# First norm by channel from a transposed input, its output kept once in DRAM and split on chip

## The chip, the cores and the metric

The kernel runs on one core of one Trainium2 chip. The metric is the device time of one execution in microseconds (us). Shown are the median of the runs and one profiled execution.

## The reference

One layer of a hybrid trunk for 128 context tokens and 2048 latent tokens of width 1024, in float32. What matters here is the start:

```python
h = rmsnorm(x, g_mix) * (1 + scale1) + shift1      # scale1, shift1 from the conditioning vector
p = h @ w_in
qkv, z, a_raw, b_raw, f = jnp.split(p, IN_SPLITS, axis=-1)
qkv = jax.nn.silu(short_conv(qkv, w_conv)).astype(jnp.float32)
```

`rmsnorm` divides each token by the root of the mean of its 1024 squares. `p` has 2576 columns: q, k, v and z with 512 each, 16 for the gates, 512 for a Fourier mixer. Behind it come a chunked gated-delta scan in both directions, the Fourier mixer, an output projection and a gated feed-forward layer.

## The kernel before

**Number format.** A float32 value is split into a high part (rounded, made by a copy on ACT) and a low part (value minus high part, on VectorE), and a product takes three matmuls: high by high, high by low, low by high. `split` (L146) is that pair.

**Layout.** Tokens come in 17 tiles of 128 (16 latent ones, tile 16 is the context), channels in 8 blocks of 128 (`KT`). A projection needs its input with channels on the partitions.

**Stage A** (`phase_a`, L355) goes over the 17 tiles, the context tile first. Per tile it loads x with tokens on the partitions (L383, SP's queue), squares and sums on ACT (`rstd`, L161, with one operation and a power of -1/2 on GpSimd), scales by the result on ACT (`norm`, L283), transposes the eight 128x128 blocks on PE into two PSUM banks, applies the modulation to each block (two of four on VectorE, two on ACT) and splits (`norm_T`, L293). High and low part are stored to DRAM in `hT[2, ...]` (L387 on ACT's queue, L388 on GpSimd's), and 48 matmuls with 528 columns of `w_in`, in two halves, give the gates' inputs and the Fourier input f. The pool `work` holds two buffers each of x, xn, h, hi, lo and f. Weights of the q and k halves are loaded and split in between (`load_halves`); the columns of the modulation come from `mod_columns` ahead of the loop.

**The q/k pass** (`qk_pass`, L550) goes over 8 blocks of 256 latent tokens in the order 0, 7, 1, 6, 2, 5, 3, 4 (`ORDER`); the text numbers blocks by their place in it, 0 to 7. Block 0 has the 128 context tokens beside it. `load_h` (L497) loads a block's high and low parts, with one token more on either side, from `hT` into eight (block 0: sixteen) of the 16 `hb` buffers, one block ahead. A block has eight steps: a projection of 24 matmuls (`project`, L524), a convolution over tokens (`conv_silu`, L535: ACT empties PSUM, VectorE adds the neighbours), and a piece of other work (the modulation of the second norm, `self.mod`; inversions of 64x64 matrices on VectorE by `fill`). Twice per block come the products of q and k.

**The v pass** (`v_pass`, L798) goes over the blocks again, block 7 first, which is still on chip, then 0 to 6, with four projections of v and two or three token tiles of z per block.

**Order.** The program's order is a wish: a scheduler places the instructions on each engine's queue by their dependencies and the buffers that are free. At run time each engine works its queue in order. Three PSUM banks take projections (`acc`), three other matmuls (`m`), two transposes (`tr`).

## Time and profile before

| | us |
|---|---|
| median of 3 runs | 2739.06 (2734.35 to 2741.23) |
| profiled execution | 2737.1 |
| its span, first to last instruction | 2735.3 |
| PE busy in the span | 2619.6 (96%) |
| VectorE (DVE) busy | 1791.5 (65%) |
| ScalarE (ACT) busy | 1412.2 (52%) |

A profile is one execution. PE is TensorE's matmuls, PEld its weight loads, DVE VectorE, ACT ScalarE, POOL GpSimd, SP the queue from which most loads are issued. Matmul records overlap, since matmuls are pipelined, so the distance between two starts is the cost of one. The granted clock is the share of full speed that TensorE was given; 1.0 is 2.4 GHz, and the lower level is 1.2 GHz. "Idle before" is the time in which an engine stood still ahead of an instruction, and the name behind the arrow is what ended it by the records.

### The profile page before, as it was taken

The numbers are of one execution on the slowest core, as the hardware profiler recorded it, in microseconds if no ns is written. First come the engines' busy times: TensorE is split into PE (matmuls) and PEld (weight loads), VectorE is DVE, ScalarE is ACT, GpSimd is POOL, SyncE is SP. The second block draws the span as 40 slices with busy tenths as digits, with TensorE's granted clock in tenths as the row PEclk, the third lists the DMA queues.
The fourth block names the chain that finished last, engine by engine and source line by source line (L and its number), as shares of the span: only waits on it lengthen the run. The fifth ranks groups of instructions, "written<-read, shape, count | busy, mean of one in ns | idle before, by whom it ended". The sixth has DMA issues, their size and how long they took to land.

```text
span 2735.3 us, 45393 instructions
## 1 busy us (share of the span) xinstructions
PE 2619.6 (96%) x16041; PEld 2382.4 (87%) x16041; DVE 1791.5 (65%) x3915; ACT 1412.2 (52%) x3108; POOL 299.5 (11%) x492
## 2 busy tenths in 40 slices
PE   6999999999999999997999999999999999999998
PEld 3898898889888778876999998889999888999986
DVE  6335978618256676667777766487776557888744
ACT  7756656423478877675433344444334444444432
POOL 0211121223200021211000000020000002000001
PEclk8999999999999999999999999999999999999999
DMA  9956788666566666645222223442222254323242
GB/s 311 307 154 197 221 229 225 190 188 187 151 175 193 180 189 180 181 145 174 78 74 70 74 82 123 139 128 74 74 71 71 88 156 140 89 85 89 89 134 93
DMA packets 436112, 396.54 MB, mean 145 GB/s; under 512 B 123084, under 2 KB 359164, under 8 KB 434284
## 3 DMA queue, kind: packets, MB, share of 16 engines
q1 hardware_dynamic: 345132, 297.65, 36.7%
q0 software_dynamic: 16624, 55.85, 6.2%
q10 hardware_dynamic: 74128, 40.13, 5.1%
q8 instruction: 127, 2.08, 0.3%
q14 instruction: 101, 0.83, 0.1%
HBM read 294.74 MB, written 98.79 MB: 144 GB/s over the span
## 4 chain that ended last, share of the span: by engine, by line
PE 73%; DMA 8%; ACT 7%; DVE 6%; issue 4%; POOL 1%; SPq 0%; ACTq 0%; DVEq 0%; POOLq 0%
PE acc L125 24%; PE acc L1304 17%; PE m L1304 16%; PE m L125 15%; DMA hb<-hT 1%; PE tr L128 1%; DMA z_s<-z_d 1%; ACT h L141 1%; ACT bd1r L141 1%; ACT bd0r L141 1%; PE tr L125 1%; ACT u L141 1%; DMA w_raw<-w_in 1%; DMA a_d<-la 1%; DMA hT<-hi 1%
## 5 line engine op out<-in xcount | busy, mean ns | idle before, releaser
L1304 PE MATMUL m<-h,wh 128*128 128x384 f32 (+1 forms) x1848 | 452.2, 327 | 5.5 <-DVE U L131 2.2
L1304 PE MATMUL acc<-h,wh 128*128 128x384 f32 (+1 forms) x1848 | 450.5, 327 | 1.9 <-ACT wh L141 1.9
L141 ACT ACTIVATE wh<-S 128x512 fp32r<-128x512 f32 x264 | 163.3, 630 | 381.4 <-DVE S L131 161.2
L1304 PEld LDWEIGHTS m<-h,wh 128*128 128x128 f32 x1848 | 326.8, 189 | 7.8 <-DVE U L131 2.9
L1304 PEld LDWEIGHTS acc<-h,wh 128*128 128x128 f32 x1848 | 326.5, 189 | 3.8 <-ACT wh L141 3.3
L125 PE MATMUL acc<-hb,w_in 128*128 128x258 f32 (+1 forms) x2304 | 324.2, 297 | 5.4 <-DMA hb<-hT 3.3
L125 PEld LDWEIGHTS acc<-hb,w_in 128*128 128x128 f32 x2304 | 310.1, 194 | 14.8 <-issue 3.5
L1304 PE MATMUL acc<-h,wl 128*128 128x384 f32 (+1 forms) x924 | 300.8, 327 | 5.6 <-DVE wl L131 5.6
L1304 PE MATMUL m<-h,wl 128*128 128x384 f32 (+1 forms) x924 | 301.3, 327 | 0.0
L131 DVE TENSOR_TENSOR wl<-S,wh 128x512 fp32r<-128x512 f32 x264 | 179.0, 687 | 5.5 <-ACT wh L141 3.5
L141 ACT ACTIVATE wh<-w_gu 128x512 fp32r<-128x512 f32 x198 | 124.4, 630 | 111.1 <-issue 42.9
L1304 PEld LDWEIGHTS acc<-h,wl 128*128 128x128 f32 x924 | 174.2, 189 | 6.2 <-DVE wl L131 6.2
L138 DVE SCALAR_TENSOR_TENSOR y<-conv_in,wconv,y 128x256 f32<-128x256 f32 (+1 forms) x216 | 97.1, 465 | 122.9 <-ACT conv_in L141 121.7
L1304 PEld LDWEIGHTS m<-h,wl 128*128 128x128 f32 x924 | 174.1, 189 | 0.2 <-DVE wl L131 0.2
L141 ACT ACTIVATE awh<-a 128x384 fp32r<-128x384 f32 x176 | 91.3, 521 | 145.6 <-PE m L125 90.7
L131 DVE TENSOR_TENSOR awl<-a,awh 128x384 fp32r<-128x384 f32 x176 | 97.3, 556 | 97.7 <-ACT awh L141 97.4
L131 DVE TENSOR_TENSOR wl<-w_gu,wh 128x512 fp32r<-128x512 f32 x198 | 135.6, 686 | 25.2 <-ACT wh L141 25.0
L131 DVE TENSOR_TENSOR S<-w_gu 128x512 f32<-128x512 f32 x132 | 91.2, 692 | 89.8 <-DMA w_gu<-w_gu 89.2
L1420 POOL DMA_DIRECT2D half_d<-gy x17 | 9.3, 548 | 1148.2 <-DVE gy L131 1147.1
L138 DVE SCALAR_TENSOR_TENSOR r<-m,nsr,pk 64x128 f32<-64x128 f32 x272 | 94.9, 349 | 50.7 <-PE m L125 46.9
L125 PE MATMUL acc<-woh,mh 128*128 128x512 f32 x272 | 112.4, 414 | 1.2 <-DVE gx L131 1.2
L138 DVE SCALAR_TENSOR_TENSOR S<-S,gl,m 128x128 f32<-128x128 f32 x272 | 82.0, 343 | 44.8 <-PE m L125 14.1
(293 smaller groups left out, 5820.6 us busy)
## 6 DMA issues: line engine op xcount, KB each, us to landing
w_gu<-w_gu SPq DMA_DIRECT2D x264, 256.0 KB
pk<-pk_d SPq DMA_DIRECT2D x68, 512.0 KB
w_dn<-w_down SPq DMA_DIRECT2D x132, 256.0 KB
hb<-hT SPq DMA_DIRECT2D x104, 258.0 KB
w_raw<-w_ada SPq DMA_DIRECT2D x32, 512.0 KB
x<-x SPq DMA_DIRECT2D x17, 512.0 KB
hT<-hi ACTq DMA_DIRECT2D x17, 512.0 KB
hT<-lo POOLq DMA_DIRECT2D x17, 512.0 KB, 5.5
```

Of the source, the lines that this page charges most:

```text
L125: self.nc.tensor.matmul(out, lhsT=lhsT, rhs=rhs, start=start, stop=stop)
L128: self.nc.tensor.transpose(out=out, in_=in_, identity=self.c("ident")[:in_.shape[0], :in_.shape[0]])
L131: (eng or self.nc.vector).tensor_tensor(out=out, in0=a, in1=b, op=op)
L138: self.nc.vector.scalar_tensor_tensor(out=out, in0=a, scalar=s, in1=b, op0=op0, op1=op1)
L141: self.nc.scalar.activation(out=out, in_=in_, func=f, **kw)
L1304: nc.tensor.matmul(o, lhsT=w_[:, ws], rhs=h_[:, k, :sub], start=start and k == i == 0, stop=k == 3 and i == 2, skip_group_check=not start)
L1420: nc.gpsimd.dma_start(self.half_d[n], tmp)
```

## The change

The host lays x out a second time as `xT`: per token tile, channels on the partitions, then block, then token. `norm_cols` loads a tile so, squares it on ACT, adds the eight blocks to one on VectorE (adds of 512, 256 and 128 columns), sums over the partitions with a one-column matmul, takes the power of -1/2 on GpSimd, forms a diagonal matrix of the results and multiplies a matrix of ones by it, which gives each token's factor on all partitions; one VectorE product applies it to all blocks. Its first part stands ahead of the matmuls of the tile before, its second part behind the first half of them. `mod_split` applies the modulation and splits; it stores h itself, once, in float32. `load_h` loads this into the place of the low part, and `split_h` makes high and low part from it on ACT and VectorE, tile by tile, at points of stage A, the q/k pass and the v pass.

```diff
--- before.py
+++ after.py
@@ -211,7 +211,7 @@
         self.wconv = const.tile([P, 12, 3], F32, name="wconv")
         nc.sync.dma_start(self.wconv, A["w_convT"])
         d = self.dram.tile
-        self.hT = d([2, P, KT, N], F32, name="hT")
+        self.hT = d([P, KT, N], F32, name="hT")
         self.f_d = d([N, 512], F32, name="f_d")
         self.z_d = d([2, N, 2, P], F32, name="z_d")
         self.pk_d = d([NC, P, 1024], F32, name="pk_d")
@@ -352,6 +352,54 @@
                 self.split(w[0][k + i], w[1][k + i], raw[:, i], *engs)
             yield
 
+    def norm_cols(self, work, t):
+
+
+        nc = self.nc
+        x = work.tile([P, KT, P], F32, tag="x", name="x")
+        nc.sync.dma_start(x, self.A["xT"][t])
+        h = work.tile([P, KT, P], F32, tag="h", name="h")
+        self.act(h.rearrange("p k t -> p (k t)"), x.rearrange("p k t -> p (k t)"), AF.Square)
+        for m in (4, 2, 1):
+            self.tt(h[:, :m], h[:, :m], h[:, m:2 * m], ALU.add)
+        ps = self.bank("tr")
+        self.mm(ps[:, 0:1], h[:, 0], self.c("ones")[:, 0:1])
+        r = self.small.tile([P, 1], F32, tag="rstd", name="rstd", bufs=4)
+        self.ts(r, ps[:, 0:1], 1.0 / D, ALU.mult, EPS, ALU.add)
+        self.rsqrt(r, r)
+        dg = work.tile([P, P], F32, tag="dg", name="dg")
+        self.ts(dg, self.c("ident"), r, ALU.mult)
+        yield
+        self.mm(ps[:, P:2 * P], self.c("ones"), dg)
+        self.tt(x, x, ps[:, P:2 * P].unsqueeze(1).to_broadcast([P, KT, P]), ALU.mult)
+        self.normed = x, h
+
+    def mod_split(self, work, x, h, r, rows):
+
+        hi = work.tile([P, KT, P], F32R, tag="hi", name="hi")
+        lo = work.tile([P, KT, P], F32R, tag="lo", name="lo")
+        for g in range(2):
+            for j in range(4):
+                k = g * 4 + j
+                a, b = (self.mod_cols[:, 0, i, k, r:r + 1] for i in range(2))
+                if j < 2:
+                    self.ts(h[:, k], x[:, k], a, ALU.mult, b, ALU.add)
+                else:
+                    self.act(h[:, k], x[:, k], AF.Identity, scale=a, bias=b)
+            ks = slice(g * 4, g * 4 + 4)
+            self.split(hi[:, ks], lo[:, ks], h[:, ks])
+        self.nc.scalar.dma_start(self.hT[:, :, rows], h)
+        return hi, lo
+
+    def split_h(self, ahead, count):
+
+        tiles, _, width = ahead
+        for _ in range(count):
+            if self.whole:
+                hi, lo = (x[:, :width] for x in tiles[self.whole.popleft()])
+                self.act(hi, lo.bitcast(F32))
+                self.tt(lo, lo.bitcast(F32), hi.bitcast(F32), ALU.subtract)
+
     def phase_a(self, wk):
 
         nc, A = self.nc, self.A
@@ -377,15 +425,14 @@
             rest = self.ada_tiles(), "m"
             self.mod = chain(self.mod_columns(1, *rest), self.mod_gate(0, *rest), self.mod_gate(1, *rest))
             qk = chain(qk, self.load_halves(wq, 0))
-            for n, t in enumerate([16] + list(range(16))):
+            order = [16] + list(range(16))
+            begin = self.norm_cols(work, order[0])
+            self.run(begin)
+            for n, t in enumerate(order):
                 rows = slice(t * P, (t + 1) * P)
-                x = work.tile([P, D], F32, tag="x", name="x")
-                nc.sync.dma_start(x, A["x"][rows])
-                hi = work.tile([P, KT, P], F32R, tag="hi", name="hi")
-                lo = work.tile([P, KT, P], F32R, tag="lo", name="lo")
-                self.norm_T(*self.norm(x, 0, work), 0, int(t == 16), hi, lo)
-                nc.scalar.dma_start(self.hT[0, :, :, rows], hi.bitcast(F32))
-                nc.gpsimd.dma_start(self.hT[1, :, :, rows], lo.bitcast(F32))
+                hi, lo = self.mod_split(work, *self.normed, int(t == 16), rows)
+                begin = self.norm_cols(work, order[n + 1]) if n < NT - 1 else iter(())
+                next(begin, None)
                 f = work.tile([P, 512], F32, tag="f", name="f")
                 for a, b in ((0, 264), (264, FW)):
                     ps = self.bank("acc")
@@ -394,6 +441,7 @@
                         self.mm(ps[:, :b - a], hi[:, k], wl[k][:, a:b], start=False, stop=False)
                         self.mm(ps[:, :b - a], lo[:, k], wh[k][:, a:b], start=False, stop=(k == KT - 1))
                     if a == 0:
+                        self.run(begin)
                         nc.vector.tensor_copy(self.ab[:, t], ps[:, :16])
                     s = max(a, 16)
                     self.act(f[:, s - 16:b - 16], ps[:, s - a:b - a])
@@ -402,6 +450,8 @@
                     next(qk, None)
                 if n == 8:
                     ahead = self.load_h(0)
+                if n > 10:
+                    self.split_h(ahead, 2)
         return wq, ahead
 
 
@@ -506,19 +556,16 @@
             segs.append((BW, NP, False, False))
             width += NP
         tiles = []
+        self.whole = deque(range(KT))
         for k in range(KT):
             if n == 0:
-                pair = []
-                for l in range(2):
-                    t = self.hb.tile([P, BW + NP], F32R, tag="hb", name="hb")
-                    nc.sync.dma_start(t.bitcast(F32)[:, :BW], self.hT[l, :, k, start:start + BW])
-                    nc.sync.dma_start(t.bitcast(F32)[:, BW:], self.hT[l, :, k, NS:])
-                    pair.append(t)
-                tiles.append(pair)
-                continue
-            t = self.hb.tile([P, 2, BW], F32R, tag="hb", name="hb")
-            nc.sync.dma_start(t.bitcast(F32), self.hT[:, :, k, start:start + BW].rearrange("l p t -> p l t"))
-            tiles.append((t[:, 0], t[:, 1]))
+                hi, lo = (self.hb.tile([P, BW + NP], F32R, tag="hb", name="hb") for _ in range(2))
+                nc.sync.dma_start(lo.bitcast(F32)[:, BW:], self.hT[:, k, NS:])
+            else:
+                t = self.hb.tile([P, 2, BW], F32R, tag="hb", name="hb")
+                hi, lo = t[:, 0], t[:, 1]
+            nc.sync.dma_start(lo.bitcast(F32)[:, :BW], self.hT[:, k, start:start + BW])
+            tiles.append((hi, lo))
         return tiles, segs, width
 
     def project(self, tiles, width, w, col):
@@ -577,6 +624,8 @@
                     ssks = [work.tile([P, 2, 4], F32, tag="ssk", name="ssk", bufs=3) for _ in groups]
                 if i % 4 < 3:
                     next(self.mod, None)
+                if n < 7 and i:
+                    self.split_h(ahead, 1 if i < 7 else 2)
                 self.fill(3.0 if n < 4 else 2.0)
                 if i % 4 == 1:
                     while late:
@@ -811,6 +860,8 @@
                 ps = self.project(tiles, width, wv, h * P)
                 self.conv_silu(work, ps, segs, 8 + h, lambda: [g[2][:, :, h] for g in groups])
                 next(self.mod, None)
+                if n != 6:
+                    self.split_h(ahead, 2)
                 self.fill(2.0)
                 if h == 1:
                     while late:
@@ -1468,8 +1519,10 @@
 def host_arrays(i):
     f = lambda a: np.ascontiguousarray(a)
     a = {k: np.asarray(v) for k, v in i.items()}
+    x = np.concatenate([a["x_sample"][0], a["x_prompt"][0]], 0)
     return {
-        "x": f(np.concatenate([a["x_sample"][0], a["x_prompt"][0]], 0)),
+        "x": f(x),
+        "xT": f(x.reshape(NT, P, KT, P).transpose(0, 3, 2, 1)),
         "condT": f(np.stack([a["c"][0], a["c_ctx"]], 0).reshape(2, KT, P).transpose(2, 1, 0)),
         "w_ada": f(a["w_ada"][0]),
         "b_adaT": f(a["b_ada"][0].reshape(48, P).T),
```

## Rows read from the trace of the kernel before

**Rows 1.** Windows by stage: us, busy us by engine (instructions), clock, DMA share, GB/s.

```profile
45.00:176.00 131.00, 118.83 (x916) 115.06 (x917) 56.42 (x130) 96.73 (x208) 36.21 (x63) 0.95 0.89 279
176.00:515.00 339.00, 324.31 (x2919) 295.08 (x2918) 259.50 (x718) 200.97 (x407) 67.87 (x89) 0.96 0.70 202
515.00:700.00 185.00, 180.99 (x1144) 162.91 (x1144) 86.26 (x211) 58.52 (x134) 49.17 (x65) 0.98 0.65 183
```

**Rows 2.** Windows in the q/k pass: PE, PEld, DVE, ACT, POOL, as above.

```profile
270.00:280.00 10.00, 8.70 (x103) 7.69 (x103) 9.13 (x7) 5.24 (x10) 2.27 (x3) 0.96 0.88 268
...
300.00:350.00 50.00, 48.28 (x522) 43.78 (x522) 45.65 (x133) 31.33 (x63) 5.79 (x6) 1.00 0.78 241
450.00:500.00 50.00, 48.24 (x468) 43.95 (x467) 47.50 (x144) 29.92 (x67) 8.48 (x8) 0.97 0.74 211
410.00:420.00 10.00, 6.47 (x73) 5.29 (x71) 1.57 (x3) 4.98 (x10) 0.78 (x1) 0.79 1.09 258
510.00:520.00 10.00, 9.03 (x50) 8.28 (x49) 9.88 (x8) 3.67 (x5) 5.76 (x10) 1.00 0.94 242
```

**Rows 3.** Grouped lines, 60 to 200 us: count, busy us, mean ns, idle before.

```profile
L125 PE MATMUL acc<-wfh,hi 128*128 128x264 f32 x248 | 72.1, 294 | 4.8 <-ACT f L141 4.8
...
L131 DVE TENSOR_TENSOR lo<-h,hi 128x512 fp32r<-128x512 f32 x30 | 20.3, 688 | 21.1 <-ACT hi L141 21.1
...
L135 DVE TENSOR_SCALAR h<-tr,mod_cols 128x128 f32<-128x128 f32 x56 | 19.8, 404 | 20.7 <-PE tr L128 17.5 <-ACT h L141 3.2
...
L141 ACT ACTIVATE xn<-x,rstd 128x512 f32<-128x512 f32 x28 | 18.8, 716 | 8.1 <-POOL rstd L131 5.8 <-DMA hT<-hi 2.2
...
L141 ACT ACTIVATE hi<-h 128x512 fp32r<-128x512 f32 x30 | 18.3, 634 | 4.5 <-DMA hb<-hT 4.4
...
L141 ACT ACTIVATE h<-x 128x1024 f32<-128x1024 f32 x13 | 13.7, 1052 | 1.6 <-DVE ab L397 1.4 <-DVE lo L131 0.2
...
L131 POOL TENSOR_TENSOR rstd<-ss,neg_half 128x1 f32<-128x1 f32 x13 | 7.8, 597 | 1.1
...
L135 DVE TENSOR_SCALAR y<-ab_abs 128x136 f32<-128x136 f32 x1 | 0.2, 233 | 1.0 <-ACT ab_abs L141 1.0
```

**Rows 4.** Timeline of PE in stage A: start, us, instruction, idle before.

```profile
62.12 0.59 PE L125 MATMUL acc<-wfh,hi 128*128 128x264 f32 x1 [3.88 <-ACT f L141]
...
67.57 1.05 PE L128 MATMUL tr<-const_all,xn 128*128 128x128 f32 x8
68.37 0.37 PE L125 MATMUL acc<-wfh,hi 128*128 128x264 f32 x1
68.58 0.28 PE L125 MATMUL acc<-wfl,hi 128*128 128x264 f32 x1
68.70 0.28 PE L125 MATMUL acc<-wfh,lo 128*128 128x264 f32 x1
...
179.00 0.28 PE L125 MATMUL acc<-wfh,lo 128*128 128x264 f32 x1
```

**Rows 5.** The page's costliest groups, and PE's timeline: other shapes.

```profile
L131 DVE TENSOR_TENSOR awl<-a,awh 128x384 fp32r<-128x384 f32 x176 | 97.3, 556 | 97.7 <-ACT awh L141 97.4
...
395.67 0.60 PE L125 MATMUL m<-inv_x,inv_bd 128*128 128x32 f32 x4 [0.84 <-PE m L125]
```

**Rows 6.** Instructions on the tensor hT: landing of GpSimd's stores of lo.

```profile
DMA to landing us min/median/max: 4.0/5.5/8.1
```

**Rows 7.** Grouped lines, 176 to 515 us: the power of -1/2 there.

```profile
L131 POOL TENSOR_TENSOR rk<-k,neg_half 128x8 f32<-128x8 f32 x8 | 15.6, 1947 | 21.6 <-DVE k L135 21.6
```

**Rows 8.** Timeline of ACT around 308 and 413 us.

```profile
308.26 1.28 ACT L141 ACT_TABLE_LOAD   x1 [4.24 <-DMA hb<-hT]
...
413.82 1.28 ACT L141 ACT_TABLE_LOAD   x1 [7.06 <-DMA hb<-hT]
```

**Rows 9.** Timeline of PE behind that.

```profile
420.02 5.53 PE L125 MATMUL acc<-hb,w_in 128*128 128x258 f32 x24
```

**Rows 10.** Timeline of PE where the v pass begins block 0.

```profile
523.30 0.95 PE L125 MATMUL acc<-hb,w_in 128*128 128x386 f32 x4 [2.34 <-DMA hb<-hT]
```

## The prediction

> **What bounds the kernel now.** I read the windows first, because shares of the whole span hide that the change lies in three stretches: stage A (first norm and the 528-column projection, 45 to 176 us), the q/k pass (to 515 us) and the v pass (to 700 us). Nothing behind 700 us is touched. In stage A PE is busy for 119 of 131 us, the DMA engines are at 0.89, ACT is at 97 and VectorE at 56 [rows 1]: PE first, ACT and DMA close behind. In the q/k pass PE is again nearly full, but in stretches so is VectorE: 45.7 of 50 us from 300 us, 47.5 from 450 us [rows 2].
>
> The steps of stage A come from the grouped lines [rows 3], their spacing on PE from the timeline [rows 4]. Records of matmuls overlap, so I take starts. The 8 transposes of a token tile start at 67.57 us and the next matmul at 68.37: 0.80 us. Matmuls of 264 columns start 0.12 us apart (68.58, 68.70). A tile needs 48 × 0.12 + 0.80 = 6.6 us of PE. From 62.12 us, where PE goes on after a gap of 3.88 us, to the last start at 179.00 us (the last 2 us shared with q/k work, so I end at 177) [rows 4] there are 248 of the 16 hi-by-wh matmuls that a tile has [rows 3], 15.5 tiles: 7.4 us per tile. The 0.8 us beyond the need are gaps, for which ACT or VectorE was late, and one start at half clock.
>
> **Stage A, what goes.** 8 transposes per tile: 17 × 0.80 = 13.6 us of PE. On ACT two scaled copies at 0.72 us [rows 3]: 17 × 1.4 = 24 us. On the queues one 512 KB store per tile (the low part, issued by POOL), 8.9 MB in all. VectorE's four modulations read SBUF instead of PSUM: 0.40 us each now, 0.23 at the nearest SBUF row, 128x136 [rows 3].
>
> **Stage A, what comes.** On PE, per tile, a 1-column and a 128-column float32 matmul with 128x128 weights. The trace has neither. The nearest are four 128x32 ones in 0.60 us, the last one's tail included [rows 5], about 0.11 apart: 0.1 us each is the lower bound; three times that for the one of 128 columns is the upper. I take 0.31 for both, nearer the lower. PE's need falls to 5.8 + 0.3 = 6.1 us. On VectorE, per tile: adds of 512, 256 and 128 columns, a product of 1024 columns, a 128x128 scaling, one small operation. The rows at 512 columns (0.688) and 384 (0.556) give 0.16 us + 1.03 ns per column [rows 3, 5]: 0.69 + 0.43 + 0.29 + 1.21 + 0.23 + 0.2 (an estimate for the small one) = 3.0 us, less 4 × 0.17 = 0.7 at the modulations. From 4 × 0.40 + 2 × 0.69 + 0.2 = 3.2 us it goes to 5.5 us per tile. That is below 6.1, so its busy time costs nothing here, hidden under PE; beyond 6.1 it would bind.
>
> What is late next is the chain of the norm. It now ends in a product that all eight blocks need, and x and h have two buffers each: the square of tile n+1 overwrites the h of tile n-1, so it waits until that tile's store has landed. Behind the first matmul of tile n-1 stand a modulation, a high part and the issue (1.3 us: 0.4 + 0.63 [rows 3] and a share of the issue), then the landing, 5.5 us at the median of the present low-part stores [rows 6]: 6.8 us. From the square to the first matmul of tile n+1: 1.05 square, 1.41 adds, 0.15 matmul, 0.2 scale, 0.60 pow on POOL, 0.23 diagonal, 0.25 matmul, 1.21 product, 0.8 two modulations, 0.63 high part, which is 6.5 us, and nine handovers at 0.1 (an estimate): 7.4 us. Two tiles per 6.8 + 7.4 = 14.2 us is 7.1 us per tile. So of the 1.3 us that PE gives up, all but 0.3 becomes waiting: 16 × -0.3 = -5 us. The gap of 3.88 us may go too; I count nothing for it. Bounds: -21 if PE binds (16 × -1.3), +13 at a period of 8.2.
>
> Moved steps: the x load stands one tile earlier on SP and waits for the x of two tiles before. Behind it wait w_in loads of the q half and the hb loads of block 0, needed tens of us later; nothing. The h store stays on ACT, one per tile. POOL loses an issue.
>
> **A page against it.** The pow lies in that chain; it took 0.60 us in stage A for one element a partition [rows 3] and 1.95 us for eight in the q/k pass, where VectorE is fuller [rows 7]. The trace doesn't say whether the elements or VectorE made it longer. The Trainium skill, page "SBUF — State Buffer" (section "Who interferes with whom"), holds that a VectorE operation with two SBUF inputs keeps out a GpSimd operation that reads SBUF for the whole of its duration; the new adds and subtractions are of that kind. By that rule the pow waits for up to one of them, which is the third rival.
>
> **The q/k pass, VectorE.** Each of a block's 8 tiles comes as one float32 array; ACT makes the high part and VectorE subtracts. Block 0 is split in stage A (8 × 0.56 us of VectorE, hidden as above). Blocks 1 to 7 are split here: 56 subtractions of 258 columns at 0.16 + 0.27 = 0.43 us, 24 us. ACT's 56 copies (at most 0.63 each, its row at 512 columns [rows 3]) are hidden: ACT is at 201 of 339 us [rows 1]. Of the windows of 10 us from 170 to 520, 14 have VectorE at 9.1 or more, the first at 270 and the last at 510 [rows 2]. The pass has 64 steps in 339 us, so these hold 26 steps: between 0 (VectorE keeps ahead of PE) and 26 × 0.43 = 11 us, or 15 with a block's last two splits in one step. I take +6, the middle, since PE is full in most of them as well.
>
> **The q/k pass, loads.** A block's 2.1 MB become 1.06 MB. At 413.8 us ACT goes on after 7.06 us of idleness that the trace puts down to an hb load; its own stores, small pieces, stood in the same traffic; at 308 us the same costs 4.24 us [rows 8]. PE starves for 3.5 of 10 us, DMA at 1.09 [rows 2], and then runs 24 matmuls in 5.5 us instead of 2.9 [rows 9]. Loss by these rows: 3.5, some 5 for 48 matmuls at half pace, and 2 at 308 us (half of ACT's idleness, an estimate): 10.5. Half the bytes of one of several streams in each burst: -5, bounds 0 and -10.5. The added wait: a copy that waits for a load holds ACT's queue, and behind it stand the evictions that free PE's three accumulator banks. The loads go out when a block begins, and their splits are spread over its 8 steps, so that should wait little.
>
> **The v pass.** Block 0 is loaded when block 7's buffers come free; PE waits 2.34 us for it [rows 10]. The load halves, but 8 subtractions of 386 columns (0.56 each, 4.5 us) stand behind a full VectorE [rows 2]: between -3 and +6, taken as +2. The other 48 splits lie under PE: VectorE is at 86 of 185 us, ACT at 59 [rows 1].
>
> **Sum.** -5 + 6 - 5 + 2 = -2 us on the profiled execution's 2737.1 us (2735.3 of span, 1.8 around it). The median of the runs shown is 2.0 us above it, so the forecast is 2739 - 2 = 2737 us. A measurement can tell about 0.3%, 8 us, from no change.
>
> **Rivals.** First, PE stays the bound of stage A: stores land faster with half the traffic (4.0 us is the fastest now [rows 6]) and the engines' order hides the chain. Then -21, VectorE +3, loads -9, v pass +2: 2714 us. For it speak the full DMA engines and ACT's 24 us; against it the two buffers.
>
> Second, on the other side: the chain binds above today's pace. It decides from 2 × 7.4 - 6.8 = 8.0 us between square and first matmul. VectorE, in order and at 5.5 us a tile, can add that by putting the next tile's adds ahead of this tile's subtractions. At a period of 8.2 us: +13, the rest as forecast, 2755 us.
>
> Third, by the page's rule: 0.69 us more in each chain, 0.35 per tile, 16 × 0.35 = 6: 2743 us.
>
> Fourth, VectorE binds wherever it is full, +15 instead of +6, and the shorter loads bring 0 because other streams fill the burst: 2751 us. For it, the 47.5 of 50.
>
> Fifth, the halved bytes don't do what they should: they were hidden anyway, 2742 us.
>
> **Chances.** Forecast 0.38 (2729 to 2747), first 0.30, second 0.14, third 0.05, fourth 0.10, fifth 0.03. Faster than 2731: most of the first and the low edge of the forecast, 0.33. Slower than 2747: second, most of the fourth and the upper edge, 0.24. Within: 0.43. For 8 in 10 the range takes in the first and second but not their tails: 2712 to 2756.
>
> **What would show it.** Stage A at 126 us (now 131), a period of 7.1 us, PE gaps that end with ACT's high part or VectorE's product, VectorE near 95 us there. In the q/k pass no ACT idleness of 4 us behind hb loads, VectorE 24 us fuller, and the pass as long as before. A stage A under 115 us makes the first rival right, over 140 the second; a q/k pass longer by 10 us the fourth.

## The result, and the profile after

The kernel became slower: 2767.7 us (2763.7 to 2772.8) beside 2738.1 (2734.4 to 2741.2), a ratio of 1.0116 with a 95% interval of 1.0095 to 1.0137. The profiled execution took 2763.9 us. The forecast was 2737 with a range that ended at 2756.

Where the 27 us came from is read from four boundaries: the last matmul of stage A with `wfh` (the row under the table), the first matmul of the v pass's z (`acc<-w_in,hb`), the last of them, and the span's end.

| us | before | after | longer by |
|---|---|---|---|
| first matmul of stage A | 45.7 | 45.7 | 0.0 |
| stage A, to its last matmul | 179.0 | 204.0 | 25.0 |
| from there to the first z | 318.7 | 321.5 | 2.8 |
| from there to the last z | 221.5 | 223.6 | 2.1 |
| from there to the end | 2016.1 | 2013.0 | -3.1 |

The tile's view of `wfh` after (count, min/median/max ns, first and last start):

```profile
L125 PE MATMUL acc<-wfh,lo x272: 279/285/590, 46.7 to 204.0; 128*128 128x264 f32 x136
```

So it is stage A. The windows after, columns as in [rows 1]; below the three stretches of [rows 1] stand 30 us from the middle of stage A, and the two full stretches of the q/k pass of [rows 2]:

```profile
45.00:176.00 131.00, 105.69 (x728) 101.22 (x728) 86.88 (x207) 72.82 (x149) 16.36 (x28) 0.88 0.63 192
176.00:515.00 339.00, 317.14 (x2919) 291.27 (x2920) 257.79 (x699) 213.70 (x460) 61.31 (x80) 0.96 0.60 170
515.00:700.00 185.00, 177.06 (x1061) 156.95 (x1060) 126.52 (x345) 80.39 (x185) 44.32 (x61) 0.96 0.50 135
105.00:135.00 30.00, 25.19 (x176) 24.24 (x177) 19.18 (x46) 16.64 (x34) 2.60 (x5) 0.89 0.55 167
300.00:350.00 50.00, 45.85 (x454) 41.83 (x454) 46.43 (x136) 31.77 (x72) 11.74 (x12) 0.97 0.59 169
450.00:500.00 50.00, 47.56 (x466) 43.13 (x465) 44.83 (x115) 29.51 (x61) 9.68 (x10) 0.97 0.80 231
```

In stage A every engine has become emptier or stayed below full: PE 106 of 131 us (119 before), ACT 73 (97), the DMA engines 0.63 (0.89), VectorE 87. No engine is the bound, the clock is lower (0.88 beside 0.95), and still the stage takes longer. That is the look of a chain, not of a load. The waits of stage A after (46 to 204 us: who waited for whom, us in total, times, longest):

```profile
DVE h L131 <- ACT h L141: 30.7, 15, 4.1
ACT h L141 <- DMA hT<-h: 25.9, 13, 3.3
PE acc L125 <- ACT hi L141: 16.4, 9, 5.9
PE tr L125 <- DVE dg L135: 9.7, 6, 2.1
```

13 of the 17 squares wait for a store of h, VectorE's adds wait for the squares, PE waits for high parts and for the diagonal. The squares alone, with the issues of the stores on ACT's queue (timeline of ACT after: start, us, instruction, idle before):

```profile
107.44 0.52 ACTq L391 DMA_DIRECT2D hT<-h  x1
110.02 0.52 ACTq L391 DMA_DIRECT2D hT<-h  x1
113.58 1.06 ACT L141 ACTIVATE h<-x 128x1024 f32<-128x1024 f32 x1 [2.56 <-DMA hT<-h]
116.86 1.06 ACT L141 ACTIVATE h<-x 128x1024 f32<-128x1024 f32 x1 [2.21 <-DMA hT<-h]
124.01 0.52 ACTq L391 DMA_DIRECT2D hT<-h  x1
127.72 0.52 ACTq L391 DMA_DIRECT2D hT<-h  x1
129.93 1.06 ACT L141 ACTIVATE h<-x 128x1024 f32<-128x1024 f32 x1 [1.60 <-DMA hT<-h]
133.49 1.06 ACT L141 ACTIVATE h<-x 128x1024 f32<-128x1024 f32 x1 [2.50 <-DMA hT<-h]
...
140.89 0.52 ACTq L391 DMA_DIRECT2D hT<-h  x1
...
146.60 1.06 ACT L141 ACTIVATE h<-x 128x1024 f32<-128x1024 f32 x1 [1.39 <-DMA hT<-h]
...
159.38 0.52 ACTq L391 DMA_DIRECT2D hT<-h  x1
...
165.24 1.06 ACT L141 ACTIVATE h<-x 128x1024 f32<-128x1024 f32 x1 [1.54 <-DMA hT<-h]
...
176.56 0.52 ACTq L391 DMA_DIRECT2D hT<-h  x1
...
182.42 1.06 ACT L141 ACTIVATE h<-x 128x1024 f32<-128x1024 f32 x1 [2.27 <-DMA hT<-h]
```

This is a closed loop of two tiles: square, 10.4 us to the issue of that tile's store (113.58 to 124.01), 5.9 us to its landing, next square in the same buffer. The next rounds are 11.0 + 5.7, 12.8 + 5.9 and 11.3 + 5.9. Four rounds take 182.42 - 113.58 = 68.8 us: 17.2 for two tiles, 8.6 per tile. Over all from the third square to the seventeenth (52.00 to 182.42) it is 9.3 us per tile; in the kernel before the same squares (48.95 to 159.78) were 7.9 apart.

What lies in the 10.4 us is seen on VectorE and GpSimd. A is the tile squared at 113.58, B the one squared at 116.86 (timelines of VectorE, GpSimd and PE after):

```profile
114.68 1.48 DVE L131 TENSOR_TENSOR h<-h 128x512 f32<-128x512 f32 x3 [2.85 <-ACT h L141]
...
117.95 1.15 DVE L131 TENSOR_TENSOR h<-h 128x512 f32<-128x512 f32 x2 [1.71 <-ACT h L141]
119.02 0.15 DVE L135 TENSOR_SCALAR rstd<-tr 128x1 f32<-128x1 f32 x1
...
120.94 1.22 DVE L131 TENSOR_TENSOR x<-x,tr 128x1024 f32<-128x1024 f32 x1 [0.65 <-PE tr L125]
```

```profile
119.32 0.57 POOL L131 TENSOR_TENSOR rstd<-rstd,neg_half 128x1 f32<-128x1 f32 x1
```

```profile
116.31 0.35 PE L125 MATMUL tr<-const_all,h 128*128 128x1 f32 x2
...
124.54 0.43 PE L125 MATMUL acc<-wfh,hi 128*128 128x264 f32 x1 [0.43 <-ACT hi L141]
```

A's column sum ends on PE at 116.66, but VectorE scales it at 119.02: ahead of that stand B's first two adds, which wait for B's square, which waited for a store. These 2.4 us of another tile's waiting are in A's chain. So the two buffers don't work as two loops side by side; both tiles go round together.

### The profile page after: what moved, and what is told of

Same layout as the page of the kernel before. It is cut to its first block, busy times and chain, and to the rows that moved or that the text cites. A ratio compares the mean times of both kernels' runs of the same rounds, so it can differ in the third digit from the quotient of the medians.

```text
span 2762.1 us, 45516 instructions
## 1 busy us (share of the span) xinstructions
PE 2622.7 (95%) x15973; PEld 2384.1 (86%) x15973; DVE 1875.5 (68%) x4137; ACT 1433.5 (52%) x3177; POOL 279.9 (10%) x458
## 4 chain that ended last, share of the span: by engine, by line
PE 39%; issue 13%; ACT 4%; DMA 4%; DVE 3%; POOL 2%; ACTq 0%; SPq 0%; POOLq 0%; DVEq 0%
PE acc L1355 11%; PE m L1355 11%; PE acc L125 9%; PE m L125 8%; DMA z_s<-z_d 1%; ACT bd1r L141 1%; DMA y_f<-half_d 1%; POOL rstd L131 1%; ACT h L141 1%; ACT bd0r L141 1%; ACT u L141 1%; PE tr L128 0%; DVE ml L131 0%; DMA w_gu<-w_gu 0%; DVE x_f L138 0%
```

## The experiments

Three steps loosen the loop, one after the other; then the queues alone; then the parts of the change alone; then VectorE's adds; then the clock. "Stage A" is the time of its last matmul (179.0 before, 204.0 after). Ratios are to the kernel before.

**The squares in a tile of their own**, so that h is held only from the modulation on.

```diff
-        h = work.tile([P, KT, P], F32, tag="h", name="h")
-        self.act(h.rearrange("p k t -> p (k t)"), x.rearrange("p k t -> p (k t)"), AF.Square)
+        s = work.tile([P, KT, P], F32, tag="sq", name="sq")
+        self.act(s.rearrange("p k t -> p (k t)"), x.rearrange("p k t -> p (k t)"), AF.Square)
```

> The changed kernel, but the squares go to a tile of their own (two buffers), and h is taken only at the modulation; so a square no longer waits for the store of h from two tiles before. Theory A (the two buffers of h, held by the store, set the pace: two tiles per landing plus chain, 16.4 us in the trace after): the last matmul of stage A comes at 180 to 190 us instead of 204, and the time is 2740 to 2752 us. Theory B (VectorE's longer work in order, 5.5 us and more per tile, sets the pace, and the wait for the store only shows where ACT has nothing else to do): stage A ends at 200 us or later and the time is 2760 to 2770 us.

Measured: 1.0106 (1.0074 to 1.0137), stage A 202.2. Waits of its stage A:

```profile
ACT sq L141 <- DMA x<-xT: 30.1, 14, 3.8
```

The wait for the store is gone and the same squares wait as often for the load of x: x too has two buffers, is read until the last modulation of its tile, and then its load of 512 KB has to land. That the time stood still looks like the theory that the stores don't matter; the wait shows that one holder took the place of the other.

**And a third buffer of x.**

```diff
-        x = work.tile([P, KT, P], F32, tag="x", name="x")
+        x = work.tile([P, KT, P], F32, tag="x", name="x", bufs=3)
```

> As the run with own squares, with a third buffer of x, so that a load waits for the tile three before. Theory A with x as the next holder: a further 5 to 15 us less than with own squares alone, stage A at 6.5 to 7 us per tile, 2730 to 2742 us. If x is not what is late next: the same as with own squares alone, within 5 us. Theory B: 2760 to 2770 us.

Measured: 1.0066 (1.0045 to 1.0087), stage A 195.1, 9 us less than in the kernel after; the time lies in none of the three ranges. Its waits:

```profile
ACT sq L141 <- DMA x<-xT: 15.3, 8, 3.3
DVE ab L446 <- PE acc L125: 21.6, 11, 5.5
```

The buffers did hold the stage, but they are a part only. What VectorE now waits for is the copy of the gates behind the first half of a tile's matmuls, and behind that copy stand the next tile's steps.

**And the second part of the next tile's norm ahead of this tile's matmuls**, not behind their first half.

```diff
                 begin = self.norm_cols(work, order[n + 1]) if n < NT - 1 else iter(())
-                next(begin, None)
+                self.run(begin)
...
                     if a == 0:
-                        self.run(begin)
                         nc.vector.tensor_copy(self.ab[:, t], ps[:, :16])
```

> Norm by channel with own squares and three buffers of x (stage A ended at 195.1 us, 2754 us), with the second part of the next tile's norm (matrix of ones by the diagonal, product) placed ahead of this tile's matmuls instead of behind their first half. Theory D (in the queues in order the product stands behind the copy of the gates' inputs, which waits for PE, 21.6 us of such waits): stage A ends at 178 to 190 us, 2735 to 2748 us. If the place of that step decides nothing: 190 to 200 us, 2748 to 2758 us. If the product then stands ahead of this tile's low part and holds PE: later than 200 us.

Measured: stage A 187.4, another 8 us less; ratio 1.0071 (1.0046 to 1.0096), no better than the run before it. In the profiled execution the gain is where it was expected. In the ratio it isn't to be seen: the median fell by 5.4 us (2753.9 to 2748.5), but that of the kernel before, measured beside each, fell by 6.4 (2735.5 to 2729.1). The profile speaks for the order; what it is worth in the whole time stays open. Of the 25 us by which stage A grew, buffers and order account for 17 in these three steps (204.0 to 187.4); no run here accounts for the other 8.

**The store of f issued by ACT**: GpSimd's queue holds no issue any more that waits for f ahead of a power.

```diff
-                nc.gpsimd.dma_start(self.f_d[rows], f)
+                nc.scalar.dma_start(self.f_d[rows], f)
```

> The kernel after, with the store of f issued by ACT, which makes f, and no longer by GpSimd, where the issue waits for f ahead of the power of -1/2 (in the kernel after GpSimd stands 94 us of stage A at that issue). Chain theory (the order of the queues lengthens the chain from square to first matmul): the power leaves the queue behind the issue; in the two-tile pattern at 118 us the issue took 0.54 us directly ahead of a power, so 0.3 to 0.5 us per tile, 5 to 8 us of stage A (end of it at 196 to 199 us, 204.0 in the kernel after), ratio to before about 1.009. Rival (the stores alone and PE set the pace, GpSimd's queue costs nothing): end of stage A at 202 to 206 us, ratio 1.012.

Measured: 1.0126 (1.0091 to 1.0161), stage A 203.8. Taking the issue out of GpSimd's queue gained nothing; that part of the theory fell. The 94 us that GpSimd stood at this issue were idle time of an engine for which VectorE waited 2.8 us in all.

**And the scaling on ACT, the diagonal on GpSimd**, out of VectorE's queue, on top of the run before.

```diff
-        self.ts(r, ps[:, 0:1], 1.0 / D, ALU.mult, EPS, ALU.add)
+        self.act(r, ps[:, 0:1], AF.Copy, scale=1.0 / D, bias=EPS)
...
-        self.ts(dg, self.c("ident"), r, ALU.mult)
+        self.ts(dg, self.c("ident"), r, ALU.mult, eng=nc.gpsimd)
```

> The kernel before this one, and the two small steps of the norm taken from VectorE: the scaling of the sum (128x1) is made on ACT, the diagonal (128x128) on GpSimd, so that neither stands behind the next tile's adds in VectorE's queue. Chain theory (the next tile's adds, which wait for the square and that for a store, hold this tile's scale: some 2.5 us in the two-tile pattern at 118 us, 1.2 us per tile): the end of stage A comes another 10 to 20 us earlier, at 180 to 190 us, ratio to before 1.003 to 1.007. Rival (the wait only moves: ACT's queue holds the scale behind the next square, which waits for the same store): within 4 us of the run before it.

Measured: 1.0145 (1.0115 to 1.0176), stage A 217.2: not shorter, not the same, but 13 us longer. Its ACT timeline, and of 46 to 204 us two waits and the group of the diagonals:

```profile
163.94 1.06 ACT L141 ACTIVATE h<-x 128x1024 f32<-128x1024 f32 x1 [4.85 <-DMA hT<-h]
...
175.38 1.06 ACT L141 ACTIVATE h<-x 128x1024 f32<-128x1024 f32 x1 [4.60 <-DMA hT<-h]
```

```profile
ACT h L141 <- DMA hT<-h: 51.4, 13, 4.9
PE tr L125 <- POOL dg L135: 4.2, 3, 2.3
```

```profile
L135 POOL TENSOR_SCALAR dg<-const_all,rstd 128x128 f32<-128x128 f32 x15 | 13.3, 886 | 1.5
```

The squares no longer come in pairs: from 120.42 us on there is one in 10.4 to 11.4 us, each at the head of ACT's queue until a store lands, and behind it stand modulations that are ready (around 112 us: the product that they need ended at 111.10, the square began at 112.10, they at 113.06). The diagonal also takes longer on GpSimd, 886 ns beside 288 on VectorE in the kernel after, but PE waited less for it (4.2 us in all, 9.7 in the kernel after), so this step by itself doesn't account for the 13 us. The waits speak for the order of the queues; that VectorE's order alone cost what I put down to it is not shown, because this run put the wait into another queue.

**The norm by channel alone**: `norm_cols` and `mod_split` as in the kernel after, but high and low part stored and loaded as before, without splits in the passes.

```diff
-        self.nc.scalar.dma_start(self.hT[:, :, rows], h)
+        self.nc.scalar.dma_start(self.hT[0, :, :, rows], hi.bitcast(F32))
+        self.nc.gpsimd.dma_start(self.hT[1, :, :, rows], lo.bitcast(F32))
```

> Only the norm by channel; high and low part are both stored and both loaded as in the kernel before, nothing is split in the passes. Here h isn't stored, so the square doesn't wait for a store of h, but high and low part are held by theirs. Theory A: stage A ends at 180 to 195 us, the time is 2740 to 2757 us. Theory B: stage A ends at 200 us or later, 2758 to 2768 us. If the splits in the passes cost something, it is missing here: the q/k pass is as long as before.

Measured: 1.0130 (1.0098 to 1.0161), stage A 209.6, 15 us behind theory A's range. The new norm alone is as slow as the whole change, and no square waits for a store here. What most of them wait for is x, as in the run with own squares:

```profile
ACT h L141 <- DMA x<-xT: 15.1, 10, 3.4
```

So the store of h is one holder of the loop, but the slow pace doesn't need it: by these waits the long chain of the norm over two buffers of x gives it as well. From the end of stage A to the first z it takes 328.3 us here (318.7 before), with nothing split in that stretch, so the splits are not what costs.

**The single copy alone**: the old norm, h stored once, `load_h` and `split_h` as in the kernel after.

```diff
-                self.norm_T(*self.norm(x, 0, work), 0, int(t == 16), hi, lo)
-                nc.scalar.dma_start(self.hT[0, :, :, rows], hi.bitcast(F32))
-                nc.gpsimd.dma_start(self.hT[1, :, :, rows], lo.bitcast(F32))
+                xn, h = self.norm(x, 0, work)
+                self.norm_T(xn, h, 0, int(t == 16), hi, lo)
+                nc.scalar.dma_start(self.hT[:, :, rows], h)
```

> Only the second part: the norm with transposes as before, h stored once in float32, split on chip in the passes. Theory A: the old chain is short enough that the wait for the store of h (its squares are written over h too) costs little; stage A ends within 5 us of 179 us, the passes are 0 to 6 us longer by the splits, 2735 to 2748 us. Theory C (the splits are what costs): 2755 us or more.

Measured: 1.0023 (1.0002 to 1.0044), stage A 189.9, and from there to the first z 316.7 (318.7 before). Stage A ends 11 us later than before, where 5 were allowed; the squares wait for the stored h here as well, more briefly:

```profile
ACT h L141 <- DMA hT<-h: 9.6, 9, 1.9
```

**And there the squares written over xn, not over h**, in the first norm alone.

```diff
-        h = work.tile([P, KT, P], F32, tag="h", name="h")
-        rstd = self.rstd(x, h.rearrange("p k t -> p (k t)"))
+        if which:
+            h = work.tile([P, KT, P], F32, tag="h", name="h")
...
+        rstd = self.rstd(x, h.rearrange("p k t -> p (k t)") if which else xn)
+        if not which:
+            h = work.tile([P, KT, P], F32, tag="h", name="h")
```

> The old norm with transposes and one float32 copy of h, and the squares of the first norm are written over the tile of the scaled x instead of over h, so that nothing waits for the store of h but the modulation two tiles later. Theory A (with h held by its store, stage A ended at 189.9 us instead of 179.0): stage A ends at 177 to 183 us, and as the splits in the passes cost nothing that could be seen, the time is 2725 to 2737 us, 4 to 12 less than with the squares over h. If the store of h isn't what made stage A longer there: 2739 to 2745 us.

Measured: 2724.6 us, 0.9964 (0.9948 to 0.9981), stage A 172.3, earlier than expected. This beats both kernels. The same window as above, of this kernel:

```profile
105.00:135.00 30.00, 28.98 (x240) 28.57 (x239) 13.80 (x34) 24.48 (x54) 5.32 (x12) 1.00 0.63 189
```

PE is full at full clock, with the transposes; no square waits for a store.

**The kernel before with its squares written over xn**, the same diff, to see whether that place of the squares is the gain by itself.

> The kernel before with one line of the other: the squares of the first norm go over the tile of the scaled x instead of over h; high and low part stored and loaded as before. It tells what the run with one copy and own squares (10 us below before) owes to which of the two. If the 17 stores less and the halved loads bring it: 2731 to 2739 us, stage A ends at 176 to 182 us. If the place of the squares brings it: 2722 to 2729 us, stage A ends near 172 us.

Measured: 1.0055 (1.0037 to 1.0073), stage A 186.1. It isn't, and the time lies in neither range. The four cases:

| ratio (stage A) | squares over h | squares over xn |
|---|---|---|
| two parts stored | 1 (179.0) | 1.0055 (186.1) |
| h stored once | 1.0023 (189.9) | 0.9964 (172.3) |

Each edit alone loses, the single copy barely in the whole time; together they win. With two parts stored, the DMA engines of this stretch stay full (0.90 from 46 to 172 us, 0.67 in the fast kernel), and squares wait for loads of x:

```profile
ACT xn L141 <- DMA x<-x: 9.1, 4, 3.9
```

Full DMA engines alone are not the reason: the kernel before has them at 0.89 in the same stretch, and no square waits for x there. Why the place of the squares loses by itself stays open.

**The eight blocks summed on PE** in place of VectorE's adds, on the kernel with three buffers of x.

```diff
-        for m in (4, 2, 1):
-            self.tt(s[:, :m], s[:, :m], s[:, m:2 * m], ALU.add)
...
-        self.mm(ps[:, 0:1], s[:, 0], self.c("ones")[:, 0:1])
+        for k in range(KT):
+            self.mm(ps[:, 0:1], s[:, k], self.c("ones")[:, 0:1], start=(k == 0), stop=(k == KT - 1))
```

> Norm by channel with own squares and three buffers of x; instead of three adds on VectorE and one matmul, eight one-column matmuls sum the squares on PE (0.8 us of PE more, 1.4 us less in each tile's chain and on VectorE). Theory A (buffers and the length of the chain set the pace): stage A, which ended at 195.1 us, ends at 183 to 190 us, the time is 2740 to 2749 us. If PE's own work sets the pace by now: 2756 to 2764 us. Theory B (VectorE's load) expects as much here as theory A, so this run tells the chain and VectorE together from PE.

Measured: 1.0078 (1.0059 to 1.0098), stage A 197.0. VectorE loses 17 us (88.3 to 71.2 between 46 and 172 us) and nothing is won, since PE takes it over. Its PE timeline and windows:

```profile
118.88 0.28 PE L125 MATMUL acc<-wfh,lo 128*128 128x264 f32 x1
119.00 3.30 PE L125 MATMUL tr<-const_all,sq 128*128 128x1 f32 x28
...
122.53 0.42 PE L125 MATMUL acc<-wfl,hi 128*128 128x264 f32 x1
122.75 0.42 PE L125 MATMUL acc<-wfh,hi 128*128 128x264 f32 x1
```

```profile
105.00:135.00 30.00, 30.00 (x230) 30.00 (x229) 15.33 (x38) 16.50 (x37) 4.55 (x7) 0.89 0.48 147
```

A one-column float32 matmul is two records, 0.118 us each (3.30 / 28): eight are 1.9 us per tile, where 0.8 more was expected. PE has no gap left, and still the clock is 0.89: ahead of the row of 28 the matmuls of 264 columns start 0.12 us apart, behind it 0.22.

**The same with the gates' copy on ACT.**

```diff
-                        nc.vector.tensor_copy(self.ab[:, t], ps[:, :16])
+                        self.act(self.ab[:, t], ps[:, :16])
```

> As the run with the sum on PE (three buffers of x), with the small copy of the gates' inputs on ACT instead of VectorE, so that the next tile's product no longer stands on VectorE behind a copy that waits for PE (21.6 us of such waits with three buffers). If that order in the queue is what is late next: stage A 4 to 10 us shorter, 2732 to 2744 us. If not: the time of the run with the sum on PE, within 4 us, or longer, if ACT's queue waits in its place.

Measured: 1.0068 (1.0049 to 1.0087), stage A 197.5. Within noise of the run before; its records leave PE no gap either (123.9 of 126 us), which speaks for PE as the bound there.

**The same sum with four buffers of x and one of the squares.**

```diff
-        x = work.tile([P, KT, P], F32, tag="x", name="x", bufs=3)
+        x = work.tile([P, KT, P], F32, tag="x", name="x", bufs=4)
...
-        s = work.tile([P, KT, P], F32, tag="sq", name="sq")
+        s = work.tile([P, KT, P], F32, tag="sq", name="sq", bufs=1)
```

> As the run with the sum on PE, with four buffers of x and one of the squares. Theory A, if loads of x still hold the squares (15.3 us of waiting with three buffers): another 3 to 10 us less, 2733 to 2745 us. Theory B (VectorE): the load of VectorE is the same, so the time is that of the run with the sum on PE, within 4 us.

Measured: 1.0191 (1.0167 to 1.0214), stage A 227.6. Two things were changed at once, and a single buffer of squares is a loop of one tile: it says nothing on x.

**16 matmuls more per tile** in the kernel after, whose results nobody reads: work meant for PE's gaps.

```diff
+                pd = self.bank("m")
+                for _ in range(16):
+                    self.mm(pd[:, :264], wh[0][:, :P], wh[0][:, :264])
```

> The changed kernel with 16 matmuls per tile added whose result nobody reads (17 x 16 x 0.12 = 33 us of PE at full clock), to take up PE's idle time in stage A. If the half clock there (granted clock 0.86 to 0.89, some 17 us lost) follows from PE's idle stretches: the granted clock of stage A rises to 0.95 or more and stage A ends at 195 to 215 us although 33 us of work were added; 2755 to 2775 us. If the clock doesn't follow from the idle time: the clock stays below 0.9 and stage A ends at 222 us or later, 2780 to 2800 us.

Measured: 1.0170 (1.0149 to 1.0192), stage A 218.5. The first fence is the kernel after, the second this run, with its middle and a late stretch below, and where the added matmuls ran:

```profile
46.00:172.00 126.00, 103.37 (x715) 99.28 (x715) 83.00 (x196) 69.97 (x143) 15.00 (x26) 0.88 0.64 196
```

```profile
46.00:172.00 126.00, 112.60 (x864) 110.39 (x863) 75.98 (x179) 63.43 (x131) 14.10 (x24) 0.95 0.56 176
105.00:135.00 30.00, 29.86 (x248) 29.65 (x246) 16.30 (x41) 12.75 (x28) 3.67 (x6) 1.00 0.44 132
165.00:195.00 30.00, 24.26 (x164) 23.20 (x163) 18.52 (x47) 14.90 (x34) 4.35 (x8) 0.87 0.43 124
```

```profile
L125 PE MATMUL m<-wfh x272: 278/283/587, 40.0 to 137.7; 128*128 128x264 f32 x136
```

With 9 us more of PE work in this stretch the granted clock rises to 0.95, that of the kernel before. The scheduler placed the added matmuls early: all ran by 137.7 us, 36 of them ahead of the stage. From 105 to 135 us, with the last of them, the clock is 1.00 and PE full; from 165 us on, without them, it is 0.87 and PE as empty as in the kernel after (24.3 of 30 us, 0.89). So in this stage the half clock goes with PE's idle stretches, though not with them alone, as the run with the sum on PE shows. 33 us of matmuls (17 × 16 × 0.12) cost 14.5 us of stage A, which ends 3.5 us behind its range. PE's idle time in the stage fell from 28.3 to 20.2 us; the rest went into the time ahead of the stage and the faster clock, not separated.

## Why the prediction was wrong, step by step

**The step that failed: the chain of the norm.** The loop over the two buffers of h was foreseen; its length was not. I put two tiles at 14.2 us: 7.4 from the square to the first matmul, 1.3 more to the issue, 5.5 to the landing. Measured are 10.4 to 12.8 to the issue (8.7 forecast) and 5.7 to 5.9 to the landing: 17.2 us. Per tile that is 8.6, not 7.1: 16 × 1.5 = 24 us on a forecast of -5, so +19 of the +25. The other 6 us are what is left; the first tiles are slower than the loop's pace (10.3 us per tile from 52.00 to 113.58 us), and no run separates why.

Most single durations were right: adds 1.48 us (1.41), scaling 0.15 (0.2), power 0.57 (0.60), product 1.22 (1.21). What was missing is waiting in queues: I added the steps as if each engine stood ready. In the round from 113.58 us it is 11.0 us to the first matmul, 3.6 more than forecast. A's scaling waits 2.4 of them behind B's adds, and 0.8 are ACT's modulations, all four of which stand ahead of its first high part (1.64 us, where I had put 0.8). In the round from 146.60 us it is also PE: the column sum could start at 149.2 and starts at 151.52, the matrix of factors could at 154.28 and starts at 155.90, both behind matmuls of the projection. That chain and buffers together set the pace is shown by the three steps that loosened them, for 17 of the 25 us; how much of it each queue costs is read from these rounds and not shown by a run.

**The second rival is what happened, in the main**: VectorE has the next tile's adds ahead of this tile's steps. The rival named the subtractions; the trace has the scaling behind them. It put its point at 8.0 us from the square to the first matmul; there are 11.0 (113.58 to 124.54), with the store landed 5.4 us after that, not 6.8. Its test, a stage A over 140 us, came out at 158 by the boundaries of this section. It was priced at a period of 8.2 and given 0.14. Both were too low: the forecast had a chain within 0.6 us of this point, made of nine handovers over four engines that work in order, and I let each be free.

**A term left out: the clock.** I counted one start at half clock and took PE's need of 6.1 us at full clock. In the kernel after PE stands still in every round and the granted clock of 105 to 135 us is 0.89 (1.00 before in the same stretch). What this costs is not separated: as long as the loop is the bound, slower matmuls between two of its steps delay it only where a step of the norm waits behind them.

The Trainium skill, page "TensorE: Matmul & The Clock Gate" (section "HAM oscillation — how this bites in real kernels"), tells of a kernel in which PE's waits for loads between groups of matmuls drop the clock each time anew. The rows are of that kind, 0.88 with the pauses and 0.95 where the added matmuls fill a part of them, though PE waits here for other engines.

**The first rival, PE as the bound**, needed short waits. It is near to what the fast kernel of the table does, with other means: there PE is at 29.0 of 30 us.

**The third rival** would have had the power wait for a VectorE operation with two SBUF inputs, 0.69 us in each chain. In stage A the powers took 0.54 to 0.94 us, 0.566 at the median and 0.627 on average, against a mean of 0.597 in [rows 3]. The two longest, 0.94 at 56.58 us and 0.81 at 87.76, lie beside such operations (VectorE, then GpSimd):

```profile
87.01 1.02 DVE L131 TENSOR_TENSOR hb<-hb 128x386 fp32r<-128x386 f32 x2
```

```profile
87.76 0.81 POOL L131 TENSOR_TENSOR rstd<-rstd,neg_half 128x1 f32<-128x1 f32 x1
```

This power ends 0.54 us behind the end of the two subtractions, and 0.54 is what the shortest power takes. The power at 119.32 us took 0.57 beside an add of 128 columns from 119.14 to 119.43. The rule of the Trainium skill, page "SBUF — State Buffer" (section "Who interferes with whom"), agrees with the two long ones; beside the short add no hold is seen. The powers' excess over their median is 15 × 0.06 = 0.9 us in all, where the rival had 6: it was mis-sized.

**What held.** Costs of single operations on VectorE, after (grouped lines, 46 to 204 us):

```profile
L135 DVE TENSOR_SCALAR h<-x,mod_cols 128x128 f32<-128x128 f32 x64 | 17.8, 339 | 0.1
L131 DVE TENSOR_TENSOR h<-h 128x512 f32<-128x512 f32 x15 | 10.4, 692 | 30.7 <-ACT h L141 30.7
```

Each float32 matmul of the norm is two records on PE. From the column sum's start at 116.31 us to the next matmul's at 116.52 it is 0.21 us, and the matrix of 128 columns at 120.52 sets the next ones back by 0.22: 0.43 us per tile where I took 0.31. VectorE's modulations fell from 404 ns [rows 3] to 339, not to 233. VectorE was no bound: 87 of 131 us.

**The q/k pass**: +6 for VectorE and -5 for the loads, +1; measured +2.8, and with the old norm -2.0. In the twelve runs that have the same pass this stretch takes 316.7 to 326.1 us, so the near hit is within their scatter and in part luck; no run separates the two terms. ACT's waits for the loads went as forecast: its idleness behind hb, 4.24 and 7.06 us in [rows 8], is down to 1.8 us in all (second row), and the 56 subtractions took 419 ns each (430 forecast), 21.5 us of busy time with no more VectorE work in the full stretches (46.4 and 44.8 of 50 us; 45.7 and 47.5 in [rows 2], though the same 50 us hold other steps now). Over the whole stretch VectorE is 14.5 us fuller (242.1 to 256.6), not 24. The fourth rival's 10 us more didn't come. After, 204 to 525 us, a group and a wait:

```profile
L131 DVE TENSOR_TENSOR hb<-hb 128x258 fp32r<-128x258 f32 x56 | 21.5, 419 | 10.4 <-ACT hb L141 10.4
```

```profile
ACT hb L141 <- DMA hb<-hT: 1.8, 2, 1.3
```

**The v pass**: +2 forecast, +2.1 measured from the first z to the last; the gap of [rows 10] behind the load is gone. With the same code it takes 217.8 to 224.5 us in those runs, so this hit too is in part luck. **The fifth rival**, that the bytes don't matter, is answered by the table of four: the single copy is worth its place once nothing else holds the buffer that it stores from.

## What to carry to other kernels

When a store leaves from a buffer, everything that writes that buffer next is in a loop with the store's landing: write the loop down as buffers, chain and landing, and let nothing that isn't stored (here a scratch of squares) share the tag. A chain of small steps over four engines has to be costed with what stands ahead of each step in its queue, the next tile's steps among it, and when the margin to today's pace is smaller than two or three such waits, the slower side deserves the higher chance. When a stage has no full engine and a lower clock, look for the loop first: 33 us of added matmuls cost 14.5 us here, and two small steps moved into other queues, one of them slower there, cost 13. And expect the next holder behind the one that is removed: without the wait for the store, the load of x held the same squares about as long (30.1 us in all beside 25.9).

## What the runs showed of the hardware that was not expected

A float32 matmul of one column takes as much of PE as one of 128 columns, 0.21 us beside 0.22, and a row of them goes at 0.118 us a record. PE can be busy in all of 30 us and still be granted 0.89: behind a row of 28 such records, 3.3 us without a gap, the next matmuls of 264 columns start 0.22 us apart, where they had started 0.12 apart. That the narrow matmuls are the reason is likely, not shown. A modulation of 128x128 elements that reads SBUF takes ACT 481 ns on average, and all four of a tile stand ahead of its first high part: 1.64 us in the round at 122.33 us, where I had put 0.8.
